# Hybrid attention trunk on one core: turned probabilities in two buffers with writes of their own, and DRAM reads emitted later

## The chip, the core and the metric

The kernel runs on one core of a Trainium2 chip. The metric is device time in microseconds for one execution of the whole program. Engines are named as the profile names them: PE (TensorE matmuls) and PEld (its weight loads), DVE (VectorE), ACT (ScalarE), POOL (GpSimd), SP (SyncE, which here issues nearly every DMA).

## What is computed

Two layers, each with a pooling mixer and a latent-attention mixer in parallel, over 512 tokens plus 16 meta tokens (T = 528), width 1024, 8 heads. Cut to what matters:

```python
for l in range(DEPTH):                      # DEPTH = 2
    h = rmsnorm(h_res, norm_gain[l])
    u_pool, z_pool, c_q, c_kv, k_rope, z_mla, g_pool, g_mla = split(h @ w_in[l])
    y_pool = (pool_mix(u_pool) * silu(z_pool)) @ pool_w_up[l]
    o_mla  = mla(c_q, c_kv, k_rope, ...)    # q, k normed and rotated; per head and block of
                                            # 128 queries: p = softmax(q k^T), causal; o = p v
    y_mla  = (o_mla * silu(z_mla)) @ mla_w_up[l]
    h_res += (sigmoid(g_pool) * y_pool + sigmoid(g_mla) * y_mla) @ w_out[l]
```

## The kernel before

**The matmul stream.** Every dense product is a `Gemm` in one list (`plan`), and `stream()` walks it: chunks of up to 512 weight columns, each loaded by `wload` (DMA `raw<-win` and the like on SP, line 133; high part `whi` on ACT, line 197; low part `wlo` on DVE, line 198) and multiplied by `mm3` in three passes (lines 202, 203, 204: high x high, high x low, low x high) to keep float32 accuracy. `raw`, `whi` and `wlo` have three buffers each. In layer 0 a chunk is 24 matmuls of 264 columns, in layer 1 it is 12 of 512.

**Attention woven into it.** `go()` runs the eight heads of a layer; between their pieces `gap()` lets the stream advance by some 2.6 us of planned matmul time (`FILL`), so that PE has dense work while DVE, ACT and the DMAs prepare a head. `after(ns, fn)` runs `fn` once the stream's own clock has advanced by `ns`. `behind(a, b)` makes instruction `a` wait for `b`; with `newest[0]` that is the last matmul emitted. Each engine runs its instructions in a fixed order. That order is not the program's: the framework's planner takes, per engine, what is ready in its own timing model, and among several the one that the program emitted first. At run time an engine, SP too, waits at the head of its queue.

**One head**, `head()`, blocks i = 0 to 3 of 128 queries, block i with 16 + 128(i+1) keys:

- First half: `scores` for block 1 (272 columns) and the first `SPL` = 240 columns of block 3 into one PSUM bank `sa`; block 2 (400 columns) into `sb`. `top` (DVE, line 824) scales, masks and takes the row maximum; `expo` (ACT, line 831) exponentiates into SBUF (`pa`, `cq`). A gap; then `turn` (DVE, line 837) transposes blocks 1 and 2 in 32x32 squares into `attD`; `pv` (lines 950, 953) multiplies an earlier head's probabilities with V; a gap.
- Second half: the other 288 columns of block 3, and block 0 (144 columns, in `passes`, line 872) into a bank `sc`; `top`, `expo` and `turn` for both. Then on SP: the row sums' reciprocals to DRAM (`rdr`, line 894), the four writes `pdr<-attD` (line 899), the read `attE<-pdr` that completes the turn (line 901), the broadcast read `cq<-rdr` (line 902). An odd head also writes and reads the meta tokens' probabilities (`mdr<-cq`, line 916; three `racc<-mdr`, line 918) and POOL multiplies the gates by the reciprocals (line 906).

`attD` has one buffer of 10 x 128 columns, `attE` has two. `parts(h)` (lines 928, 929) splits `attE` into high and low for `pv`; it comes four gaps after head h, with head h+1 in between. `prep` (lines 791 to 801) makes the next head's query and key tiles, largely by small SBUF-to-SBUF DMAs on SP.

PSUM has three banks with tag `S` (`sa`, `sb`, `sc` of a head in turn) and four with tag `mm`. `WARM` = 8 matmuls on ones (line 155) precede the first real matmul. `halves()` lends buffers, among them `attD` and `attE`, as scratch for squares before attention starts.

Of the kernel before, what the change touches and what calls it, by code (L numbers as in the profile page):

```python
# [9 lines left out]
F32 = mybir.dt.float32  # L10
F32R = mybir.dt.float32r
# [7 lines left out]
P = 128  # L19
DEPTH = 2  # L20
D = 1024
SEQ = 512
NM = 16
T = SEQ + NM
HALF = T // 2
# [28 lines left out]
RESERVE = ("gm3", "gm3")  # L54
LAG = 2000.0
TAIL = (9000.0, 9000.0)
SPL = 240
RET = 12500.0
WARM = 8
NB = 10  # L60


def block(i, j):
    return 2 * i + j if j < 2 else 1 if i == 2 else 6 + j
# [14 lines left out]
def trunk(ctx, tc, xT, xrow, mrow, pos, win, wkr, wqb, wkb, wvb, wgr, wpu, wmu, wout, gains, const, yT):  # L79
    nc = tc.nc  # L80
    pe, act, dve, gp, sp = nc.tensor, nc.scalar, nc.vector, nc.gpsimd, nc.sync
# [11 lines left out]
    def nm(s):  # L93
        uid[0] += 1
        return f"{s}_{uid[0]}"

    def slot(tag, dt=F32, bufs=1, w=W):
        return sl.tile([P, w], dt, tag=tag, name=nm(tag), bufs=bufs)
# [1 line left out]
    def tmp(w=W):  # L100
        return tp.tile([P, w], F32, tag="tmp", name=nm("tmp"), bufs=3)

    def att(tag):
        return sl.tile([P, NB * P], F32 if tag == "D" else F32R, tag=f"att{tag}", name=nm(f"att{tag}"), bufs=1 if tag == "D" else 2)

    def wide():
        return tp.tile([P, NB * P], F32R, tag="th", name=nm("th"), bufs=2)

    def halves():
        for k in range(4, 8):  # L110
            for a, b in FULL:
                yield xb[:, k, a:b]
        for tag in "DE":
            t = att(tag)
            for a in range(4):
                yield t[:, HALF * a:HALF * a + HALF].bitcast(F32)

    def mmt():
# [2 lines left out]
    def sct():  # L121
        return pp.tile([P, 512], F32, tag="S", name=nm("S"), bufs=3)
# [84 lines left out]
    newest = [None]  # L207
# [60 lines left out]
    def after(ns, fn):  # L268
        pend.append((clk[0] + ns, fn))
        pend.sort(key=lambda e: e[0])  # L270
# [32 lines left out]
    def behind(ins, other):  # L303
        tc.add_manual_dep(ins.ins, other.ins.name,
                          mybir.DependencyInfo(mybir.DependencyClass.Sync, mybir.DependencyReason.DATA))
# [35 lines left out]
    class Layer:  # L341
# [463 lines left out]
        def head(self, h, kq, prev):  # L805
            kh, kl, qh, ql = kq
            odd = h % 2
            nqs = self.nqs
            pa, pb, pc = slot("pa", w=416), slot("cq8"), slot("cq10")
            bia = sm.tile([P, 5], F32, tag="bia", name=nm("bia"), bufs=2)  # L810
            rs = sm.tile([P, 5], F32, tag="rs", name=nm("rs"), bufs=2)
            if odd == 0:
                self.pm = sm.tile([P, 4, 32], F32, tag="pm", name=nm("pm"), bufs=2)
                self.rb = slot("cq11")
            pm, rb = self.pm, self.rb
            blocks = att("D")
            grid = blocks.rearrange("p (b s r) -> p b s r", b=4, s=NB)

            def scores(i, out, a, b):
                q0 = NM + P * i  # L820
                return mm3(out, qh[:, q0:q0 + P], ql[:, q0:q0 + P], kh[:, a:b], kl[:, a:b], True, True)

            def top(i, c, sv, mask):
                return dve.tensor_tensor_reduce(out=sv, in0=sv, in1=mask, scale=nqs[:, i, h:h + 1], scalar=3e38,  # L824
                                                op0=ALU.add, op1=ALU.min, accum_out=bia[:, c:c + 1])

            def causal(n):
                return maskw[:, 512 - n:]

            def expo(i, c, sv, pv):  # L830
                act.activation(pv, sv, AF.Exp, scale=-1.0, bias=bia[:, i:i + 1], accum_out=rs[:, c:c + 1])  # L831

            def turn(i):
                gp.tensor_copy(pm[:, i, 16 * odd:16 * odd + 16], pt[i][:, 0:NM])  # L834
                for j, n in ((0, i + 1),) if i in (0, 1, 3) else ((0, 2), (2, 1)):
                    k = block(i, j)
                    ins = dve.transpose(grid[:, :, k:k + n, :].rearrange("p b s r -> p s b r"), pt[i][:, NM + P * j:NM + P * (j + n)])  # L837
                    if i in (1, 2):
                        behind(ins, newest[0])

            pt = [pa[:, 0:144], pa[:, 144:416], pb[:, 0:400], pc[:, 0:T]]
            sa = sct()
            s1, s3 = sa[:, 0:272], sa[:, 272:272 + SPL]
            scores(1, s1, 0, 272)
            scores(3, s3, 0, SPL)
            top(1, 1, s1, causal(272))
            top(3, 4, s3, maskw[:, 0:SPL])
            sb = sct()
            s2 = sb[:, 0:400]
            scores(2, s2, 0, 400)  # L850
            top(2, 2, s2, causal(400))
            expo(1, 1, s1, pt[1])
            expo(2, 2, s2, pt[2])
            if h == 1:
                self.spread_rope(1)
            if odd == 0 and h + 2 < H:
                self.spread_k(h // 2 + 1)
            self.gap()
            turn(1)
            turn(2)  # L860
            self.pv(prev)
            if h == 2:
                self.rope_keys(1)
            if odd and h + 1 < H:
                behind(self.keys(h // 2 + 1), newest[0])
            self.gap()
            sc = sct()
            s0, s4 = sc[:, 0:144], sc[:, 144:144 + T - SPL]
            scores(3, s4, SPL, T)

            def passes(out, q0, n):
                return [lambda k=k, q=q, x=x: pe.matmul(out, q[:, q0], x[:, 0:n], start=k == 0, stop=k == 2)
                        for k, (q, x) in enumerate(((qh, kh), (qh, kl), (ql, kh)))]

            todo = passes(s0, slice(NM, NM + P), 144)
            if not self.last:
                sm_ = sc[0:NM, 432:432 + NM]
                todo += passes(sm_, slice(0, NM), NM)
            for fn in todo:
                fn()  # L880
            if not self.last:
                dve.tensor_add(self.smeta[:, h, :], sm_, cst[0:NM, C_MM:C_MM + NM])
            top(3, 3, s4, causal(T - SPL))
            top(0, 0, s0, causal(144))
            dve.tensor_tensor(out=bia[:, 3:4], in0=bia[:, 3:4], in1=bia[:, 4:5], op=ALU.min)
            expo(3, 4, s3, pt[3][:, 0:SPL])
            expo(3, 3, s4, pt[3][:, SPL:T])
            expo(0, 0, s0, pt[0])
            turn(3)
            turn(0)  # L890
            dve.tensor_add(rs[:, 3:4], rs[:, 3:4], rs[:, 4:5])
            dve.reciprocal(rs[:, 0:4], rs[:, 0:4])
            row = rdr[self.l][h]
            sp.dma_start(row.rearrange("a (p i) -> p (a i)", i=4), rs[:, 0:4])
            got = att("E")
            n = NB * 32
            via = pdr[h % 2]
            for a in range(4):
                sp.dma_start(via[:, n * a:n * a + n].rearrange("(b k) x -> k b x", k=32),
                             blocks[32 * a:32 * a + 32, :].rearrange("p (b x) -> p b x", x=n))  # L900
            sp.dma_start(got.bitcast(F32), via)
            sp.dma_start(rb[64 * odd:64 * odd + 64, 0:512], row.partition_broadcast(64))
            if odd == 1:
                self.meta_turn(pm)
                z = self.zms[h // 2][:, NM:T].rearrange("p (i q) -> p i q", i=4)
                gp.tensor_mul(z, z, rb[:, 0:512].rearrange("p (q i) -> p i q", i=4))  # L906
            return h, got

        def meta_turn(self, pm):
            t = slot("cq9", F32R)  # L910
            f, hi, lo = t[:, 0:P], t[:, P:2 * P], t[:, 2 * P:3 * P]
            dve.transpose(f.bitcast(F32), pm.rearrange("p i r -> p (i r)"))
            split(hi, lo, f.bitcast(F32), 0, P)
            self.mt = slot("racc", F32R)
            via = mdr[0]
            sp.dma_start(via, t[:, P:3 * P].bitcast(F32))
            for g, c in ((0, 0), (32, 1), (64, 0)):
                sp.dma_start(self.mt[g:g + 32, 0:512].bitcast(F32).rearrange("p (a x) -> p a x", a=4),
                             via[:, P * c:P * c + P].rearrange("(a r) x -> r a x", a=4))

        def parts(self, prev):
            if prev is None:
                return None
            h, got = prev
            hi, f = wide(), got.bitcast(F32)
            for a in (0, NB * 64):
                b = a + NB * 64
                behind(act.activation(hi[:, a:b], f[:, a:b], AF.Copy), newest[0])  # L928
                dve.tensor_sub(got[:, a:b], f[:, a:b], hi[:, a:b].bitcast(F32))  # L929
            return h, hi, got  # L930
# [333 lines left out]
```

## Time and profile before

| | |
|---|---|
| median of 3 runs | 771.3 us (768.76 to 771.66) |
| the profiled execution's own time | 770.3 us |
| its span, first to last instruction | 768.5 us |
| DVE, ACT, POOL busy | 537.7, 393.3, 141.1 us |
| DMA | 113.03 MB, 48% of 16 engines' time |
| attention of layer 0, of layer 1 | from about 177 to 316 us, from about 564 to 695 us |

Times are microseconds from the span's start unless marked ns. Line numbers (L199) are lines of the kernel before. In a timeline row stand start, duration, engine and line, operation, output<-inputs, tile shape and count; in brackets the engine's idle time just before and what ended it. `SPq` marks an instruction of SP's queue, and its duration is the time that issuing took, not the transfer. In a row of the waits stand total, number and longest. A matmul's duration in a row includes the pipeline's depth: the distance from one start to the next is what it costs.

### The profile page before, as it was taken

How to read it: one execution, taken by the hardware profiler on the slowest of the kernel's cores; microseconds unless marked ns; L12 is line 12 of the kernel's file. 1: busy time of each engine (PE TensorE's matmuls, PEld its weight loads, DVE VectorE, ACT ScalarE, POOL GpSimd, SP SyncE). 2: the span in 40 equal slices, each digit the busy share in tenths (PEclk: the TensorE clock that was granted, in tenths of full speed). 3: DMA queues.
4: the chain of work that ended last, by engine and by line, in shares of the span. 5: the costliest groups of instructions: out<-in, count | busy, mean ns of one | idle time of the engine just before them, and what ended most of it. 6: DMA issues, size and time to landing. Idle time of an engine off the chain costs nothing.

```text
span 768.5 us, 14306 instructions
## 1 busy us (share of the span) xinstructions
PE 757.2 (99%) x5028; PEld 689.0 (90%) x5028; DVE 537.7 (70%) x1211; ACT 393.3 (51%) x864; POOL 141.1 (18%) x187
## 2 busy tenths in 40 slices
PE   9999999999999899999999999999999999999998
PEld 9999999999989899999997898887788788788887
DVE  4588787358889887684366477774578799776832
ACT  5755655545556555543255445455445556554320
POOL 2026404000101010052130264030001110112400
PEclk9999999999999999999999999999999999999999
DMA  7532323336765667425542323234457677673363
GB/s 261 181 109 84 100 80 104 118 124 165 200 201 164 179 201 204 141 83 147 177 143 93 114 83 100 80 89 132 127 158 197 197 207 206 187 214 105 121 196 108
DMA packets 77204, 113.03 MB, mean 147 GB/s; under 512 B 15382, under 2 KB 36246, under 8 KB 77132
## 3 DMA queue, kind: packets, MB, share of 16 engines
q1 hardware_dynamic: 76988, 111.86, 48.4%
q8 instruction: 39, 0.64, 0.3%
q14 instruction: 33, 0.27, 0.1%
q10 hardware_dynamic: 144, 0.26, 0.1%
HBM read 89.76 MB, written 15.86 MB: 137 GB/s over the span
## 4 chain that ended last, share of the span: by engine, by line
PE 85%; DVE 6%; DMA 5%; SPq 1%; issue 1%; ACT 1%; DVEq 0%; ACTq 0%
PE mm L202 26%; PE mm L204 25%; PE mm L203 25%; DMA raw<-win 2%; PE S L202 2%; PE S L204 2%; PE S L203 2%; DVE wlo L198 1%; DVE S L824 1%; DMA kh<-kh 1%; DMA pdr<-attD 1%; PE S L528 1%; PE o L950 1%; PE o L953 1%; DMA mdr<-cq 1%
## 5 line engine op out<-in xcount | busy, mean ns | idle before, releaser
L202 PE MATMUL mm<-hh,whi 128*128 128x264 f32 (+2 forms) x1072 | 338.9, 318 | 5.9 <-ACT whi L197 4.0
L204 PE MATMUL mm<-hh,wlo 128*128 128x264 f32 (+2 forms) x1072 | 338.4, 318 | 0.2 <-DVE wlo L198 0.2
L203 PE MATMUL mm<-hl,whi 128*128 128x264 f32 (+2 forms) x1072 | 337.9, 316 | 0.0
L198 DVE TENSOR_TENSOR wlo<-raw,whi 128x512 fp32r<-128x512 f32 (+2 forms) x242 | 172.5, 715 | 108.5 <-ACT whi L197 103.3
L197 ACT ACTIVATE whi<-raw 128x512 fp32r<-128x512 f32 (+2 forms) x242 | 144.4, 600 | 181.2 <-PE mm L203 126.8
L202 PEld LDWEIGHTS mm<-hh,whi 128*128 128x128 f32 x1072 | 202.7, 189 | 20.2 <-ACT whi L197 4.9
L203 PEld LDWEIGHTS mm<-hl,whi 128*128 128x128 f32 x1072 | 202.8, 189 | 12.4
L204 PEld LDWEIGHTS mm<-hh,wlo 128*128 128x128 f32 x1072 | 202.2, 189 | 12.7 <-DVE wlo L198 0.6
L834 POOL COPY pm<-cq 128x16 f32<-128x16 f32 x32 | 13.3, 416 | 216.5 <-ACT cq L831 216.5
L824 DVE CUSTOM_DVE_ANT_0 S<-S,maskw,nqs 128x240 f32<-128x240 f32 (+4 forms) x80 | 38.3, 499 | 2.3 <-PE S L204 1.7
L642 POOL TENSOR_TENSOR racc<-racc,tmp 128x264 f32<-128x264 f32 (+1 forms) x15 | 14.3, 957 | 134.8 <-ACT tmp L641 134.8
L1025 POOL TENSOR_TENSOR tmp<-tmp,xb 128x264 f32<-128x264 f32 (+1 forms) x24 | 27.1, 1142 | 55.2 <-DVE tmp L1023 53.3
L831 ACT ACTIVATE cq<-S,bia 128x400 f32<-128x400 f32 (+2 forms) x48 | 24.4, 512 | 25.0 <-DVE bia L824 11.9
L202 PE MATMUL mm<-cq,whi 128*128 128x264 f32 (+1 forms) x108 | 34.8, 322 | 0.0
L203 PE MATMUL mm<-th,whi 128*128 128x264 f32 (+1 forms) x108 | 34.7, 321 | 0.0
L202 PE MATMUL mm<-u,whi 128*128 128x264 f32 (+1 forms) x108 | 34.6, 321 | 0.0
L204 PE MATMUL mm<-cq,wlo 128*128 128x264 f32 (+1 forms) x108 | 34.6, 322 | 0.0
L203 PE MATMUL mm<-cq,whi 128*128 128x264 f32 (+1 forms) x108 | 34.6, 321 | 0.0
L204 PE MATMUL mm<-u,wlo 128*128 128x264 f32 (+1 forms) x108 | 34.5, 319 | 0.0
L837 DVE STREAM_TRANSPOSE attD<-cq 128x256 f32<-128x256 f32 (+2 forms) x48 | 21.3, 467 | 12.7 <-DMA pdr<-attD 7.2
L906 POOL TENSOR_TENSOR u<-u,cq 128x512 f32<-128x512 f32 x8 | 12.4, 1552 | 76.4 <-DMA cq<-rdr 26.9
L929 DVE TENSOR_TENSOR attE<-attE,th 128x640 fp32r<-128x640 f32 x32 | 25.1, 809 | 0.5 <-ACT th L928 0.5
(297 smaller groups left out, 1304.7 us busy)
## 6 DMA issues: line engine op xcount, KB each, us to landing
raw<-win SPq DMA_DIRECT2D x143, 256.0 KB, 3.3
pdr<-attD SPq DMA_DIRECT2D x64, 160.0 KB, 3.1
attE<-pdr SPq DMA_DIRECT2D x16, 640.0 KB, 4.9
raw<-wout SPq DMA_DIRECT2D x32, 256.0 KB, 2.9
raw<-wpu SPq DMA_DIRECT2D x16, 256.0 KB, 2.7
raw<-wmu SPq DMA_DIRECT2D x16, 256.0 KB, 2.5
raw<-wqb SPq DMA_DIRECT2D x12, 256.0 KB, 2.6
xb<-xT SPq DMA_DIRECT2D x8, 264.0 KB, 5.6
```

The source lines that it names most:

```text
L197: act.activation(hi[:, :n], raw[:, :n], AF.Copy)
L198: dve.tensor_sub(lo[:, :n], raw[:, :n], hi[:, :n].bitcast(F32))
L202: first = pe.matmul(out, wh, xh, start=start, stop=False)
L203: pe.matmul(out, wh, xl, start=False, stop=False)
L204: newest[0] = pe.matmul(out, wl, xh, start=False, stop=stop)
L642: self.acc_last = gp.tensor_add(self.acc[:, a:b], self.acc[:, a:b], t[:, :b - a])
L824: return dve.tensor_tensor_reduce(out=sv, in0=sv, in1=mask, scale=nqs[:, i, h:h + 1], scalar=3e38, op0=ALU.add, op1=ALU.min, accum_out=bia ...
L831: act.activation(pv, sv, AF.Exp, scale=-1.0, bias=bia[:, i:i + 1], accum_out=rs[:, c:c + 1])
L834: gp.tensor_copy(pm[:, i, 16 * odd:16 * odd + 16], pt[i][:, 0:NM])
L837: ins = dve.transpose(grid[:, :, k:k + n, :].rearrange("p b s r -> p s b r"), pt[i][:, NM + P * j:NM + P * (j + n)])
L929: dve.tensor_sub(got[:, a:b], f[:, a:b], hi[:, a:b].bitcast(F32))
L1025: gp.tensor_add(t[:, :b - a], t[:, :b - a], self.am[m][:, a:b])
```

## The change

- `attD` is split: `attC` (6 x 128 columns: blocks 0, 1, 2) and `attD` (4 x 128: block 3), one buffer each. Each is written to DRAM by four DMAs of its own (`away(0)`, `away(1)`), so eight writes per head for the same bytes. `away(0)` stands in the first half, behind `turn(1)`, `turn(2)` and `turn(0)`.
- Block 0 is scored in the first half: its three matmuls go into bank `sa`, beside blocks 1 and 3, after the `top` of both in program order. `SPL` falls from 240 to 96, so block 3 is cut into 96 and 432 columns.
- The reads back (`attE<-pdr`, `cq<-rdr`, then POOL's multiplication) are emitted by `after(BACK)`, 5200 ns of stream time later, each behind the newest matmul. An odd head's meta write is emitted 2600 ns later and its three reads 7800 ns later.
- `WARM` is 9. `halves()` lends other buffers, `attE` twice.

```diff
-SPL = 240
+SPL = 96
+BACK = 5200.0
-WARM = 8
+WARM = 9
...
-        for tag in "DE":
-            t = att(tag)
-            for a in range(4):
+        for tag, n in (("C", 6), ("D", 4), ("E", NB), ("E", NB)):
+            t = att(tag, n)
+            for a in range(n * P // HALF):
...
-                self.rb = slot("cq11")
-            pm, rb = self.pm, self.rb
-            blocks = att("D")
-            grid = blocks.rearrange("p (b s r) -> p b s r", b=4, s=NB)
+            pm = self.pm
+            blocks, grid = [], []
+            for tag, n in (("C", 6), ("D", 4)):
+                blocks.append(att(tag, n))
+                grid.append(blocks[-1].rearrange("p (b s r) -> p b s r", b=4, s=n))
+            n, via = NB * 32, pdr[h % 2]
+
+            def away(i):
+                x0, x1 = ((0, 192), (192, n))[i]
+                for a in range(4):
+                    sp.dma_start(via[:, n * a + x0:n * a + x1].rearrange("(b k) x -> k b x", k=32),
+                                 blocks[i][32 * a:32 * a + 32, :].rearrange("p (b x) -> p b x", b=4))
...
-                    if i in (1, 2):
+                    if i != 3:
                         behind(ins, newest[0])
...
-            s1, s3 = sa[:, 0:272], sa[:, 272:272 + SPL]
+            s1, s3, s0 = sa[:, 0:272], sa[:, 272:272 + SPL], sa[:, 368:512]
             scores(1, s1, 0, 272)
             scores(3, s3, 0, SPL)
             top(1, 1, s1, causal(272))
             top(3, 4, s3, maskw[:, 0:SPL])
+            for fn in passes(s0, slice(NM, NM + P), 144):
+                fn()
             sb = sct()
             s2 = sb[:, 0:400]
             scores(2, s2, 0, 400)
             top(2, 2, s2, causal(400))
+            top(0, 0, s0, causal(144))
             expo(1, 1, s1, pt[1])
             expo(2, 2, s2, pt[2])
+            expo(0, 0, s0, pt[0])
...
             turn(1)
             turn(2)
+            turn(0)
+            away(0)
             self.pv(prev)
...
-            s0, s4 = sc[:, 0:144], sc[:, 144:144 + T - SPL]
+            s4 = sc[:, 0:T - SPL]
             scores(3, s4, SPL, T)
...
-            expo(0, 0, s0, pt[0])
             turn(3)
-            turn(0)
...
+            got = []
+            away(1)
             sp.dma_start(row.rearrange("a (p i) -> p (a i)", i=4), rs[:, 0:4])
-            got = att("E")
-            n = NB * 32
-            via = pdr[h % 2]
-            for a in range(4):
-                sp.dma_start(via[:, n * a:n * a + n].rearrange("(b k) x -> k b x", k=32),
-                             blocks[32 * a:32 * a + 32, :].rearrange("p (b x) -> p b x", x=n))
-            sp.dma_start(got.bitcast(F32), via)
-            sp.dma_start(rb[64 * odd:64 * odd + 64, 0:512], row.partition_broadcast(64))
             if odd == 1:
                 self.meta_turn(pm)
-                z = self.zms[h // 2][:, NM:T].rearrange("p (i q) -> p i q", i=4)
-                gp.tensor_mul(z, z, rb[:, 0:512].rearrange("p (q i) -> p i q", i=4))
+
+            def back():
+                got.append(att("E"))
+                behind(sp.dma_start(got[0].bitcast(F32), via), newest[0])
+                if odd == 0:
+                    self.rb = slot("cq11")
+                rb = self.rb
+                behind(sp.dma_start(rb[64 * odd:64 * odd + 64, 0:512], row.partition_broadcast(64)), newest[0])
+                if odd == 1:
+                    z = self.zms[h // 2][:, NM:T].rearrange("p (i q) -> p i q", i=4)
+                    gp.tensor_mul(z, z, rb[:, 0:512].rearrange("p (q i) -> p i q", i=4))
+
+            after(BACK, back)
             return h, got
...
-            self.mt = slot("racc", F32R)
             via = mdr[0]
-            sp.dma_start(via, t[:, P:3 * P].bitcast(F32))
-            for g, c in ((0, 0), (32, 1), (64, 0)):
-                sp.dma_start(self.mt[g:g + 32, 0:512].bitcast(F32).rearrange("p (a x) -> p a x", a=4),
-                             via[:, P * c:P * c + P].rearrange("(a r) x -> r a x", a=4))
+
+            def back():
+                self.mt = slot("racc", F32R)
+                for g, c in ((0, 0), (32, 1), (64, 0)):
+                    ins = sp.dma_start(self.mt[g:g + 32, 0:512].bitcast(F32).rearrange("p (a x) -> p a x", a=4),
+                                       via[:, P * c:P * c + P].rearrange("(a r) x -> r a x", a=4))
+                    behind(ins, newest[0])
+
+            after(BACK / 2, lambda: behind(sp.dma_start(via, t[:, P:3 * P].bitcast(F32)), newest[0]))
+            after(1.5 * BACK, back)
```

More of the change, by code (lines that the diff above doesn't have):

```diff
@@ L101, in tmp, with att @@
         return tp.tile([P, w], F32, tag="tmp", name=nm("tmp"), bufs=3)
-    def att(tag):
-        return sl.tile([P, NB * P], F32 if tag == "D" else F32R, tag=f"att{tag}", name=nm(f"att{tag}"), bufs=1 if tag == "D" else 2)
+    def att(tag, n=NB):
+        return sl.tile([P, n * P], F32 if tag != "E" else F32R, tag=f"att{tag}", name=nm(f"att{tag}"), bufs=1 if tag != "E" else 2)
     def wide():
@@ L835, in turn @@
                 for j, n in ((0, i + 1),) if i in (0, 1, 3) else ((0, 2), (2, 1)):
-                    k = block(i, j)
-                    ins = dve.transpose(grid[:, :, k:k + n, :].rearrange("p b s r -> p s b r"), pt[i][:, NM + P * j:NM + P * (j + n)])
-                    if i in (1, 2):
+                    g, k = grid[i // 3], block(i, j) - 6 * (i // 3)
+                    ins = dve.transpose(g[:, :, k:k + n, :].rearrange("p b s r -> p s b r"), pt[i][:, NM + P * j:NM + P * (j + n)])
+                    if i != 3:
                         behind(ins, newest[0])
@@ L847, in head, with passes @@
             top(3, 4, s3, maskw[:, 0:SPL])
+            def passes(out, q0, n):
+                return [lambda k=k, q=q, x=x: pe.matmul(out, q[:, q0], x[:, 0:n], start=k == 0, stop=k == 2)
+                        for k, (q, x) in enumerate(((qh, kh), (qh, kl), (ql, kh)))]
+            for fn in passes(s0, slice(NM, NM + P), 144):
+                fn()
             sb = sct()
@@ L867, in head @@
             sc = sct()
-            s0, s4 = sc[:, 0:144], sc[:, 144:144 + T - SPL]
+            s4 = sc[:, 0:T - SPL]
             scores(3, s4, SPL, T)
[L871 to L875, printed above, removed]
             if not self.last:
                 sm_ = sc[0:NM, 432:432 + NM]
[L878 to L881, printed above, removed]
+                for fn in passes(sm_, slice(0, NM), NM):
+                    fn()
                 dve.tensor_add(self.smeta[:, h, :], sm_, cst[0:NM, C_MM:C_MM + NM])
             top(3, 3, s4, causal(T - SPL))
-            top(0, 0, s0, causal(144))
             dve.tensor_tensor(out=bia[:, 3:4], in0=bia[:, 3:4], in1=bia[:, 4:5], op=ALU.min)
@@ L924, in parts @@
             h, got = prev
+            got = got[0]
             hi, f = wide(), got.bitcast(F32)
```

## The prediction

> **What bounds the kernel now.** I begin with busy time by engine and the list of what PE waited for.
>
> ```profile
> PE 757.2 (99%) x5028; PEld 689.0 (90%) x5028; DVE 537.7 (70%) x1211; ACT 393.3 (51%) x864; POOL 141.1 (18%) x187
> ```
> ```profile
> PE mm L202 <- ACT whi L197: 4.0, 3, 1.9
> PE mm L202 <- DVE tmp L655: 1.8, 1, 1.8
> ```
>
> PE is the bound: nothing off PE can save more than PE's holes. The second view has almost all of them: three waits for a weight's high part, 4.0 us in all, the longest 1.9 and the others about 1.0 each, and one of 1.8 us for an eviction. All four lie in attention. Next, the stretches around the two longest, with PE's granted clock as the column after the engines:
>
> ```profile
> 257.00:270.00 13.00, 10.95 (x75) 10.44 (x74) 11.76 (x30) 7.78 (x19) 0.39 (x2) 0.87 0.58 168
> 594.00:608.00 14.00, 12.11 (x50) 9.93 (x50) 9.98 (x25) 5.99 (x14) 3.22 (x5) 0.88 0.71 203
> ```
> ```profile
> 601.10:604.40 3.30, 3.30 (x11) 2.84 (x10) 3.30 (x11) 3.22 (x10) 0.99 (x2) 0.50 0.27 81
> ```
>
> After each of the two the clock falls: the means 0.87 over 13 us and 0.88 over 14 us are 1.7 us lost each, and the third row shows it at 0.50, PE busy throughout. So the four holes cost 4.0 + 1.8 + 2 x 1.7 = 9.2 us. *A rule beside it:* the Trainium skill, "TensorE: Matmul & The Clock Gate", section "Why this matters for your kernels", warns only of idle gaps over about 3 us. By it these holes would cost 5.8 us and the sum below would end 3.4 us higher; the 0.50 after holes of 1.8 and 1.9 us says otherwise, and I go by the row.
>
> Why are they there? SP's queue before the longest (PE stops at about 598.5):
>
> ```profile
> 583.66 0.34 SPq L133 DMA_DIRECT2D raw<-win  x1
> ```
> ```profile
> 588.61 2.01 SPq L899 DMA_DIRECT2D pdr<-attD  x4
> ```
> ```profile
> 593.18 0.34 SPq L901 DMA_DIRECT2D attE<-pdr  x1
> 593.57 0.52 SPq L801 DMA_DIRECT2D qhl<-q  x1
> 594.20 1.50 SPq L918 DMA_DIRECT2D racc<-mdr  x3
> 595.74 0.51 SPq L801 DMA_DIRECT2D qhl<-q  x1
> 596.30 1.83 SPq L133 DMA_DIRECT2D raw<-win  x3
> ```
> ```profile
> 599.89 0.63 ACT L197 ACTIVATE whi<-raw 128x512 fp32r<-128x512 f32 x1 [6.60 <-DMA raw<-win]
> ```
>
> For 12.6 us no weight is loaded, then three in a row: their buffers had been free. SP was busy issuing an odd head's burst (writes, reads back, the meta exchange, the next head's queries) and standing at its head. ACT sits 6.60 us without weights, and PE runs dry. The stall for an eviction comes the other way, over DVE:
>
> ```profile
> SPq L902 <- DMA rdr<-rs: 17.3, 10, 2.8
> SPq L918 <- DMA mdr<-cq: 17.1, 6, 3.6
> ```
> ```profile
> SPq L901 <- DMA pdr<-attD: 9.2, 12, 1.3
> ```
> ```profile
> DVE attD L837 <- DMA pdr<-attD: 9.8, 5, 3.0
> ```
> ```profile
> 257.49 0.64 DVE L837 STREAM_TRANSPOSE attD<-cq 128x256 f32<-128x256 f32 x2 [2.56 <-PE S L872]
> ```
>
> SP stands 17.3 + 17.1 + 9.2 = 43.6 us before reads whose writes have not landed. DVE stands 9.8 us because the one `attD` is still being written out; just before the 1.8 us hole it stood 2.56 us at the same instruction.
>
> **The change part by part.**
>
> *The two buffers.* Blocks 0 to 2 are written out in the first half, so the next head's first `turn` finds `attC` long free, and block 3's buffer has half a head to drain. The 12.4 us of DVE's waiting go; the hole behind them (1.8, and 1.7 of clock) goes with it. Next late there would be `wlo`, which has DVE's freed time. DVE, ACT and POOL get the same number of instructions over the same columns; block 0's `top`, `expo` and `turn` only swap halves with 144 columns of block 3.
>
> *The later reads.* 16 `attE`, 16 `cq` and 24 `racc` reads and 8 meta writes are emitted after the weight loads of two gaps, so the planner prefers those loads. I count the three weight holes as gone: 4.0 + 1.7 us. The new waits on PE stand in SP's queue before these reads; behind them wait weight loads and `prep`'s copies. Each names a matmul that was newest at emission, two gaps after the head, which is about where the next head's first scores stand. In the rows above and below these run at 588.5 and the read is issued at 593.18: its writes land later than that matmul ends. I take nothing for the new waits; above, they keep SP standing as today, and one hole of 1.0 us stays in each layer, 2 us.
>
> *Four more writes per head.*
>
> ```profile
> pdr<-attD SPq DMA_DIRECT2D x64, 160.0 KB, 3.1
> attE<-pdr SPq DMA_DIRECT2D x16, 640.0 KB, 4.9
> ```
>
> The bytes stay, in pieces of 96 and 64 KB, and only the reads wait for their landing, 3.1 us today. From the row at 588.61, 0.50 us of SP each: 64 x 0.50 = 32 us over both layers, against 43.6 us of standing that the later reads can save. Half of them go out in the first half, away from the burst. Nothing on PE, as long as no load is pushed out by over its lead; if that cover goes, a weight hole returns (1.0 us, or 1.9 with 1.7 of clock).
>
> *Matmuls.* Start to start, in layer 1:
>
> ```profile
> 588.46 0.27 PE L204 MATMUL S<-kh,qhl 96*128 96x240 f32 x1
> 588.57 0.35 PE L202 MATMUL S<-kh,qhl 96*128 96x400 f32 x1
> 588.75 0.34 PE L203 MATMUL S<-kl,qhl 96*128 96x400 f32 x1
> ```
> ```profile
> 593.14 0.39 PE L204 MATMUL mm<-hh,wlo 128*128 128x512 f32 x1
> 593.37 0.30 PE L202 MATMUL S<-kh,qhl 96*128 96x288 f32 x1
> 593.50 0.30 PE L203 MATMUL S<-kl,qhl 96*128 96x288 f32 x1
> ...
> 593.77 0.23 PE L872 MATMUL S<-kh,qhl 96*128 96x144 f32 x1
> 593.84 0.28 PE L872 MATMUL S<-kl,qhl 96*128 96x144 f32 x1
> 593.95 0.27 PE L872 MATMUL S<-kh,qhl 96*128 96x144 f32 x1
> 594.06 0.44 PE L202 MATMUL mm<-hh,whi 128*128 128x512 f32 x1
> ```
>
> 240 columns cost 0.11 us, 288 0.13, 400 0.18, 512 0.23; 144 cost 0.07 once and then 0.11, no less than 240, so narrow passes are bounded by something other than columns. 432 lies between 400 and 512: 0.197. The 96 has no row: below, 0.045 by columns (0.05 per 112 from 400 to 512); above, 0.11 as a follow-on 144. Per head, three passes each: 240 + 288 + 144 took 0.33 + 0.39 + 0.29 = 1.01 us; 96 + 144 + 432 take 0.33 + 0.29 + 0.59 = 1.21 at the upper end and 1.02 at the lower. Times 16: +0.2 to +3.2 us. The 144 is the nearest row, so I take +2.8.
>
> *The ninth warm-up matmul.*
>
> ```profile
> 1.05 3.78 PE L155 MATMUL wps<-ones 128*128 128x128 f32 x16 [1.05 <-DVE na L754]
> 5.18 0.99 PE L202 MATMUL S<-hh,th 128*128 128x264 f32 x2 [0.35 <-ACT hh L364]
> ```
>
> Eight take 3.4 us up to their successor, 0.43 each; a ninth fills the 0.35 us hole and runs over by 0.1. Bounds: +0.43 if nothing hides it; -1.7, one half-clock stretch as above, if an unbroken start brought the full clock one stretch earlier. I take +0.1.
>
> *Sum.* -9.2 + 2.8 + 0.1 = -6.3. Every engine's order is planned anew, and I leave one hole of about 0.8 us in: -5.5. The profiled execution took 770.3 us (span 768.5), 1.0 below the median of 771.3; from the median, **765.8 us**.
>
> **The rivals.**
>
> *PE waits for DVE at block 0 (slower).* Block 0's matmuls now write the bank in which `top` of blocks 1 and 3 works, and come after both. Does the program order work on one bank whose columns differ? Yes:
>
> ```profile
> 624.84 0.51 DVE L824 CUSTOM_DVE_ANT_0 S<-S,maskw,nqs 128x272 f32<-128x272 f32 x1
> ...
> 627.77 0.46 DVE L824 CUSTOM_DVE_ANT_0 S<-S,maskw,nqs 128x240 f32<-128x240 f32 x1
> ```
> ```profile
> 628.39 0.49 ACT L831 ACTIVATE pa<-S,bia 128x272 f32<-128x272 f32 x1 [1.66 <-DVE bia L824]
> ```
>
> Block 1's `expo` reads columns finished at 625.4 and still sits 1.66 us until block 3's `top`, in the same bank, is done. The Trainium skill ("PSUM — Partial Sum Buffer", section "PSUM bank collisions raise a hardware error") asks just that: guard by bank, not by address. So PE, in fixed order with the whole stream behind those three matmuls, will wait for DVE once per head where the planner has placed them too early. For: in these rows the second `top` ends 2.9 us behind the first, whose columns were scored together; such lags are long and uneven. Against: PE depends on DVE for every `wlo` and many evictions, and the list of its waits has one DVE entry of weight, 1.8 us, so the planner's places mostly hold. It decides from 0.35 us a head, which eats the gain; at 0.9 us a head, 14.4 us: **780 us**.
>
> *The reads come too late for `parts` (slower).*
>
> ```profile
> 670.29 0.34 SPq L901 DMA_DIRECT2D attE<-pdr  x1
> ```
> ```profile
> 675.54 1.37 ACT L928 ACTIVATE th<-attE 128x640 fp32r<-128x640 f32 x2
> ```
>
> That read, 4.9 us in the median, had 5.25 us. If a read falls 2 to 3 us further back, ACT stands with `whi` queued behind it; at 0.7 us of it per head on PE, 11 us: **777 us**. Against: today's reads wait for writes, not for their place.
>
> *The change doesn't do what it says.* As shown, the due point is past before the writes land, so the reads may keep their place in the burst, while 32 us of writes are added. Then only DVE's hole goes: -3.5 + 2.8 + 0.1, **770.7 us**.
>
> **How the numbers follow.** Forecast 0.50 (759 to 768: all holes gone and 96 columns at the lower end, up to one long hole left); no later reads 0.25 (768 to 774); PE waiting for DVE 0.15 and late reads 0.10 (774 to 783). A measurement of this kernel tells about 0.5% from no change, so faster is below 767.4 and slower above 775.2. Faster: 0.48 of the forecast and 0.04 of the third, 0.52; slower: 0.20 of the two slower ones and 0.03 of the third, 0.23; same: 0.25. Range for 8 in 10: 758, with the clock bound of the warm-up in it, to 779.
>
> **What would show it.** Right: no clock of 0.50 in attention, PE's waits for `whi` and `tmp` under 2 us in all, DVE's wait at L837 for `pdr` gone, loads of `raw` between the writes and the read of one head, SP's waits before the reads well under 43.6 us. The matmul term: the start-to-start distance of the 96. Wrong: PE's waits name `top` before the 144 columns, or ACT waits for `attE`, or SP shows over 10 us without a `raw` load again.

## The result and the profile after

The changed kernel takes 774.94 us in the median (772.98 to 778.06), the kernel before 770.36 us beside it: a ratio of **1.0069, 95% interval 1.0052 to 1.0085**, slower by 4.0 to 6.5 us. 765.8 us was forecast. The profiled executions took 770.3 us before and 778.06 us after, at the upper end of its runs, so the traces differ by more (7.8 us) than the medians do (4.6).

Busy time by engine, on the page of after:

```profile
PE 760.3 (98%) x5030; PEld 686.9 (88%) x5030; DVE 538.3 (69%) x1211; ACT 394.4 (51%) x864; POOL 142.9 (18%) x187
```

PE's idle time is span less busy: 768.5 - 757.2 = 11.3 us before, 776.3 (the span of after) - 760.3 = 16.0 after. So of the 7.8 us, 3.1 are more busy time and 4.7 more idle time. Where they lie shows when both traces are read at the same matmul of the stream. When attention of layer 0 begins, the changed kernel is 2.2 us ahead (its clock rose earlier at the start of that execution, see the last section); when that attention has ended it is 1.0 ahead, at the end of layer 1's 7.8 behind. So 8.8 of the 10.0 us that attention loses are lost in layer 1, where PE's idle time grew from 3.1 to 7.2 us.

What PE waited for (total, times, longest). In rows of the changed kernel and of the experiments, line numbers are lines of that version: L203 is here what L202 was before.

```profile
PE mm L203 <- ACT whi L198: 4.4, 5, 2.0
PE S L203 <- DMA kh<-cq: 3.4, 3, 1.7
PE S L203 <- issue: 1.6, 1, 1.6
...
PE o L973 <- DVE attE L949: 1.0, 1, 1.0
PE S L205 <- DMA qhl<-q: 0.6, 1, 0.6
```

The eviction's 1.8 us is gone, the weight holes are not (4.0 before, 4.4 now), and a kind of wait that hardly stood in the list of before (0.6 us) is new: scores wait for `prep`'s key and query copies, DMAs in SP's queue. (`issue` means that the profile shows nothing that PE waited for in those 1.6 us.) So SP comes next. Its timeline around the longest `whi` hole, in layer 0, and PE's row behind it:

```profile
254.86 1.05 SPq L134 DMA_DIRECT2D raw<-win  x2
256.01 0.50 SPq L798 DMA_DIRECT2D kl<-kl  x1
256.56 3.09 SPq L825 DMA_DIRECT2D pdr<-attC  x4
...
260.86 0.55 SPq L800 DMA_DIRECT2D kh<-cq  x1
...
264.88 3.23 SPq L825 DMA_DIRECT2D pdr<-attD  x4
...
269.46 0.32 SPq L911 DMA_DIRECT2D attE<-pdr  x1
...
274.25 1.62 SPq L134 DMA_DIRECT2D raw<-win  x3
```
```profile
263.94 0.54 PE L203 MATMUL S<-kh,qhl 96*128 96x272 f32 x2 [1.69 <-DMA kh<-cq]
```
```profile
278.11 0.39 PE L203 MATMUL mm<-hh,whi 128*128 128x264 f32 x1 [2.03 <-ACT whi L198]
```

No weight is loaded from the second of the pair at 254.86 until 274.25, 18.8 us from issue to issue. The key copy of 260.86, for which PE waits until 263.94, stands behind the four writes of `attC` (3.09 us of issuing); four of `attD` follow (3.23 us), and the next loads come so late that PE stops for 2.03 us at 278.11. The same stretch of the kernel before:

```profile
251.15 0.57 SPq L133 DMA_DIRECT2D raw<-win  x1
251.83 0.39 SPq L899 DMA_DIRECT2D pdr<-attD  x1
...
252.75 1.58 SPq L899 DMA_DIRECT2D pdr<-attD  x3
...
257.12 0.54 SPq L133 DMA_DIRECT2D raw<-win  x1
257.83 0.34 SPq L901 DMA_DIRECT2D attE<-pdr  x1
258.23 3.28 SPq L133 DMA_DIRECT2D raw<-win  x2
```

There loads stand on both sides of the writes. In 6 of layer 1's 8 heads the writes of after do not even stand in two places. One head on four engines (PE, ACT, DVE, SP):

```profile
571.43 0.29 PE L203 MATMUL S<-kh,qhl 128*128 128x272 f32 x1
...
578.24 0.35 PE L203 MATMUL S<-kh,qhl 128*128 128x432 f32 x1
...
578.82 0.23 PE L859 MATMUL S<-kh,qhl 128*128 128x144 f32 x1
```
```profile
581.09 0.47 ACT L840 ACTIVATE pa<-S,bia 128x272 f32<-128x272 f32 x1
```
```profile
582.38 0.62 DVE L846 STREAM_TRANSPOSE attC<-pa 128x256 f32<-128x256 f32 x2
583.12 0.67 DVE L846 STREAM_TRANSPOSE attD<-cq 128x512 f32<-128x512 f32 x1
```
```profile
588.56 2.00 SPq L825 DMA_DIRECT2D pdr<-attC  x4
590.66 1.86 SPq L825 DMA_DIRECT2D pdr<-attD  x4
```

Block 0's 144 columns were to be scored in the first half. They run at 578.82, behind block 3's 432, in the second; so they do in 9 of the 16 heads. Block 1's `expo` shares a bank with them and waits: 9.7 us behind its scores here, 11.3 in the median against 6.7 before. Both buffers are filled at the same moment, and all eight writes leave in a row. Between the loads at 583.56 and 599.49 lie 15.9 us, at this place 12.6 before. The writes are not the whole of it: in between SP also stands, ahead of a key copy, for 3.7 us (2.7 before):

```profile
SPq L800 <- DMA kh<-kh: 3.7, 1, 3.7
```

The clock (the column after the engines) at the two places shown of before, then of the half-speed stretch in the second, and behind the 2.03 us hole:

```profile
257.00:270.00 13.00, 11.31 (x89) 10.89 (x88) 11.80 (x31) 7.17 (x18) 0.39 (x2) 1.00 0.56 162
594.00:608.00 14.00, 11.75 (x50) 9.61 (x49) 9.62 (x27) 7.85 (x20) 2.36 (x5) 0.88 0.82 226
602.10:605.50 3.40, 3.40 (x11) 3.02 (x11) 2.56 (x8) 3.23 (x10) 0.64 (x3) 0.50 0.78 245
```
```profile
278.20:281.60 3.40, 3.31 (x25) 3.10 (x26) 3.03 (x9) 3.40 (x12) 0.71 (x3) 1.00 0.44 137
```

### The profile page after: what moved, and what is told of

It reads as the page before. It is cut to its first block, busy times and chain, and to the rows that moved or that the text cites. A ratio compares the mean times of both kernels' runs of the same rounds, so it can differ in the third digit from the quotient of the medians.

```text
span 776.3 us, 14420 instructions
## 1 busy us (share of the span) xinstructions
PE 760.3 (98%) x5030; PEld 686.9 (88%) x5030; DVE 538.3 (69%) x1211; ACT 394.4 (51%) x864; POOL 142.9 (18%) x187
## 4 chain that ended last, share of the span: by engine, by line
PE 84%; DMA 8%; DVE 3%; SPq 2%; ACT 1%; issue 1%; POOL 0%; DVEq 0%; ACTq 0%
PE mm L205 25%; PE mm L203 25%; PE mm L204 25%; DMA raw<-win 4%; PE S L203 2%; PE S L204 2%; PE S L205 2%; DMA kh<-cq 1%; DMA kh<-kh 1%; PE o L973 1%; PE o L970 1%; DMA attE<-pdr 1%; DVE wlo L199 1%; PE S L529 1%; ACT whi L198 1%
## 5 line engine op out<-in xcount | busy, mean ns | idle before, releaser
L203 PE MATMUL mm<-hh,whi 128*128 128x264 f32 (+2 forms) x1072 | 337.9, 317 | 4.4 <-ACT whi L198 4.4
L199 DVE TENSOR_TENSOR wlo<-raw,whi 128x512 fp32r<-128x512 f32 (+2 forms) x242 | 174.8, 726 | 118.7 <-ACT whi L198 113.6
L203 PEld LDWEIGHTS mm<-hh,whi 128*128 128x128 f32 x1072 | 201.7, 189 | 19.1 <-ACT whi L198 6.2
L204 PEld LDWEIGHTS mm<-hl,whi 128*128 128x128 f32 x1072 | 201.9, 188 | 12.6
L833 DVE CUSTOM_DVE_ANT_0 S<-S,maskw,nqs 128x144 f32<-128x144 f32 (+4 forms) x80 | 38.2, 497 | 3.8 <-PE S L859 1.8
L203 PE MATMUL mm<-cq,whi 128*128 128x264 f32 (+1 forms) x108 | 34.8, 322 | 0.0
L203 PE MATMUL mm<-u,whi 128*128 128x264 f32 (+1 forms) x108 | 34.6, 320 | 0.0
L948 ACT ACTIVATE th<-attE 128x640 fp32r<-128x640 f32 x32 | 21.9, 730 | 12.3 <-DMA attE<-pdr 8.0
```

Source lines behind the costliest of these rows:

```text
L199: dve.tensor_sub(lo[:, :n], raw[:, :n], hi[:, :n].bitcast(F32))
L203: first = pe.matmul(out, wh, xh, start=start, stop=False)
L204: pe.matmul(out, wh, xl, start=False, stop=False)
```

## The experiments

Ratios are to the kernel before, measured beside each version on the same chip. In the expectations, "burst theory", later "SP theory", is that SP's long run of issues at a head's end costs the time; its rivals are the narrower matmuls, the later reads, the order of work in one bank, and chance in the planner's new order. "Without a load" means from one weight load's issue to the next within attention, its first 20 us or so aside, where every version has a long one.

**Undoing one part of the changed kernel.** First the place of block 0's matmuls in program order, ahead of the two `top`s that work in their bank:

```diff
             scores(3, s3, 0, SPL)
+            for fn in passes(s0, slice(NM, NM + P), 144):
+                fn()
             top(1, 1, s1, causal(272))
             top(3, 4, s3, maskw[:, 0:SPL])
-            for fn in passes(s0, slice(NM, NM + P), 144):
-                fn()
```

> The changed kernel with block 0's three matmuls emitted ahead of the two tops that work in the same bank, so that PE need not come back to that bank after DVE. Burst theory (block 0 sits in a bank with blocks 1 and 3, the planner places its matmuls late, the first half's writes slide to the second half's, and SP issues eight writes in a row while key copies and weight loads wait): the four first-half writes come some microseconds ahead of the others again, the PE waits for key copies go, ratio to before about 1.000 (0.996 to 1.003). Matmul rival (narrower passes, 2.2 us of PE time, plus chance): stays near 1.006. Late-reads rival (reads emitted 5.2 us later starve the parts step): stays near 1.006.

Measured: 777.12 us, 1.0018 (0.9989 to 1.0048). Block 0 is late in one head, and block 1's `expo` lags 7.0 us:

```profile
573.16 0.21 PE L203 MATMUL S<-kh,qhl 96*128 96x96 f32 x1
...
573.43 0.30 PE L855 MATMUL S<-kh,qhl 96*128 96x144 f32 x1
```
```profile
576.86 0.49 ACT L840 ACTIVATE pa<-S,bia 128x272 f32<-128x272 f32 x1 [0.45 <-DVE bia L833]
```

The 144 columns stand right behind the 96, and some 0.5% comes back. Next, in the changed kernel, all reads and the meta exchange are emitted at once again (`back()` in place of `after(BACK, back)`, without `behind`):

> The changed kernel with every read back and the meta exchange emitted at once, as before the change. Late-reads rival: the gain comes back, ratio to before about 1.001, ACT's waits for attE (8.0 us in the changed kernel) gone. Burst theory: the burst of eight writes plus reads is as long or longer, ratio 1.006 to 1.012. Matmul rival: about 1.006.

Measured: 785.32 us, 1.0137 (1.0092 to 1.0181), PE waiting 7.0 us for `whi`. So the later reads are not what the change costs; here it is dearer without them.

**One part alone in the kernel before.** The later reads; the scoring (`SPL` = 96, block 0 in bank `sa`, one `attD`, four writes); the two buffers with eight writes at the head's end:

> The kernel before with only the later emission of the reads and of the meta exchange; one attD, four writes, block 0 in the second half. Late-reads rival: most of the loss is here, ratio 1.004 to 1.007. Burst theory: no loss, 0.995 to 1.001, since weight loads go ahead of the reads. Matmul rival: 1.000.

> The kernel before with only the scoring moved: block 0 in the first half beside blocks 1 and 3, SPL 96, one attD, four writes, reads at once. Matmul rival: 2.2 us of PE, ratio 1.003, and most of the loss if the rest of it is chance. Burst theory: 2.2 us plus a little, 1.002 to 1.005: without the four extra writes the late first half costs less than in the changed kernel. Late-reads rival: 1.000 to 1.003.

> The kernel before with the two buffers and eight writes alone; block 0 in the second half, so all eight writes stand at the head's end, reads at once. SP theory: 32 us more of issuing in the burst, ratio 1.003 to 1.010, with waits for whi and key copies. If only the bank order matters: 0.996 to 1.001, as DVE no longer waits for attD.

Measured: 775.09 us, 1.0001 (0.9974 to 1.0029); 787.0 us, 1.0162 (1.0119 to 1.0205); 789.25 us, 1.0175 (1.014 to 1.0211). Scoring and eight writes each cost more alone than the whole change, and more than either had been expected to. A part of it is the clock: in the profiled execution with the eight writes it was granted at 0.50 for 34.1 us of attention in all, in that with the scoring for 13.7, in the kernel before for 6.8. The scoring with `a_bank`'s order on top of it:

> As d_score_only (scoring moved alone, ratio 1.016 there), with block 0's three matmuls emitted ahead of the two tops of their bank. Burst theory in its new form (the bank order is what makes the moved scoring dear: exp of block 1 lags its scores by 11 us instead of 7): the ratio falls to 1.002 to 1.007, the lag to about 7 us. Matmul rival (narrow passes plus chance): stays at 1.010 or above.

Measured: 784.0 us, 1.0101 (1.0055 to 1.0147), with block 1's lag down from 11.4 to 7.3 us. The bank's order is a part of the scoring's cost, 0.6% (the two intervals overlap), and not the whole.

**Are the writes' issues the cost?** `attC`'s four writes go to POOL's queue, without and with the order of `a_bank`:

```diff
-                    sp.dma_start(via[:, n * a + x0:n * a + x1]
+                    (sp if i else gp).dma_start(via[:, n * a + x0:n * a + x1]
```

> The changed kernel with the four writes of attC issued from POOL's queue instead of SP's, so SP issues 64 DMAs less; the scoring order is the changed kernel's. SP theory (what costs is the length of SP's burst): ratio to before 0.998 to 1.003, PE's waits for key copies and whi fall by half. Bank-order-only theory (the late first half itself starves PE): stays at 1.005 to 1.009.

> a_bank (block 0's matmuls ahead of the tops, 1.002) with the four writes of attC issued from POOL: SP issues five per head, as in the kernel before. SP theory: 0.990 to 0.998, as m_bank_two. If POOL's queue is a poor place for them (its copies of the meta columns stand behind, as i_pool's 1.012 suggests): 1.002 to 1.010.

Measured: 784.04 us, 1.0117 (1.0081 to 1.0152), and 775.37 us, 0.9993 (0.9969 to 1.0017). Fewer issues on SP alone bring nothing; SP theory missed in the first and fell just short in the second. Then the DRAM buffer is laid out anew, so that a half's write is one DMA from all 128 partitions and the read is four pieces:

```diff
-                for a in range(4):
-                    sp.dma_start(via[:, n * a + x0:n * a + x1].rearrange("(b k) x -> k b x", k=32),
-                                 blocks[i][32 * a:32 * a + 32, :].rearrange("p (b x) -> p b x", b=4))
+                sp.dma_start(via.rearrange("(b p) x -> p b x", b=4)[:, :, x0:x1],
+                             blocks[i].rearrange("p (b x) -> p b x", b=4))
```

with `a_bank`'s order, in the changed kernel, in the kernel before (one write, four reads), and in that with the later reads:

> a_bank (the changed kernel, block 0's matmuls ahead of the tops; 1.002) with the DRAM buffer laid out so that each half's write is one DMA and the read is four: six issues per head on SP instead of nine. SP theory: 0.993 to 0.999, better than both kernels. If SP's issues are not what costs: 1.000 to 1.004, as a_bank.

> The changed kernel, bank order untouched, with the DRAM buffer laid out so that each half's write is one DMA and the read four: six issues per head on SP instead of nine. SP theory (the number of issues in the burst at a head's end): 0.996 to 1.002. Bank-order theory (late first half is what costs, whatever SP issues): 1.005 to 1.010. If both are needed: about 1.003.

> The kernel before with the same DRAM layout: one write and four reads, five issues as before. A control: SP theory says 0.997 to 1.003, since the number of issues stands. If the layout itself is the gain of m_bank_two (0.990), for instance because the turned blocks land sooner, 0.988 to 0.995.

> c_reads_only (the kernel before with only the later reads, 1.000) with that layout: one write, four reads, later. Without the moved scoring it saves its 2.3 us of narrow passes. If layout and later reads are what helps in m_bank_two: 0.985 to 0.992. If the two buffers are needed: 0.996 to 1.002.

Measured: 768.6 us, 0.9903 (0.9866 to 0.9941); 772.95 us, 0.9976 (0.9952 to 1.0); 769.92 us, 0.9908 (0.9874 to 0.9943); 765.9 us, **0.985 (0.9813 to 0.9887)**. Four pairs, each 0.9 to 1.5% faster than its partner without the layout (1.0018, 1.0069, 1, 1.0001). PE's waits for `whi` are 0.0, 1.9, 0.4 and 0.0 us in the four, against 0.2, 4.4, 4.0 and 8.0 in the partners. The mere number of issues isn't what the layout saves: the third issues five DMAs per head for this exchange, as the kernel before does, and SP theory had put it at 0.997 to 1.003. The last is the fastest version and beats both kernels. SP in it, at the place that the prediction showed of before:

```profile
583.48 0.53 SPq L898 DMA_DIRECT2D pdr<-attD  x1
...
587.00 0.58 SPq L134 DMA_DIRECT2D raw<-win  x1
...
588.20 1.84 SPq L905 DMA_DIRECT2D attE<-pdr  x4
...
590.61 1.06 SPq L134 DMA_DIRECT2D raw<-win  x2
```

One write of 0.53 us, and loads between it and its read. Is it the single write or the reads in pieces? The same layout, but the write again in four DMAs (each one group of 128 columns from all partitions):

> The kernel before with the regrouped DRAM buffer, but the write stays four DMAs (now one per group of 128 columns, each from all 128 partitions) and the read is four: eight issues of SP where the version with one write had five. If the gain of 0.9% came from the reads in four pieces with loads between them, or from writes that touch all 128 partitions, it stays here (0.989 to 0.994). If it came from the write being one issue, so that the last byte leaves 1.5 us earlier, this one is at 0.998 to 1.006, SP standing less but issuing 2 us more per head.

Measured: 775.61 us, 1.0038 (1.0016 to 1.006), 1.3% above the version with one write, which is more than any edit that does nothing moved the time (next paragraph). The reads in pieces bring nothing; the single write does.

**What does any new order bring?** Every edit makes the planner order all engines anew. Two versions of the kernel before that do the same work (one with a ninth warm-up matmul), the changed kernel with its warm-up undone, and both kernels at a second `FILL`:

> The kernel before with FILL at 2600 and 2510 in place of 2620 and 2530: the same work, and the stream's chunks stand at slightly other places between the pieces of attention, so every engine gets a new order. If the differences of the parts (-0.9 to +1.75%) are what any new order brings by chance, this one lies as far out: below 0.99 or above 1.01. If they come from the mechanisms named, this one lies between 0.995 and 1.005, with waits for whi on PE of 2 to 7 us.

> The kernel before with a ninth warm-up matmul alone. By the prediction's term +0.1 us, at most +0.43 (1.0000 to 1.0006); -1.7 us (0.998) if it brought the full clock a stretch earlier. If a new order alone moves the time, it lies outside 0.995 to 1.005.

> The changed kernel with eight warm-up matmuls as before the change. If the ninth is worth nothing, the changed kernel's 1.007 stays (1.004 to 1.010). If the 0.7% is the chance of one order, it lies anywhere from 0.995 to 1.02.

> The kernel before with FILL at 2640 and 2550: the other direction from the version with 2600 and 2510, which took 1.0075. If the FILL of before stands in a narrow optimum, this one is at 1.003 to 1.010 too; if a new order moves the time to either side by chance, it may lie below 1 (0.993 to 1.01).

> The changed kernel with FILL at 2640 and 2550. If the change has a cost of its own, this one stands 0.5 to 1% above the kernel before with the same FILL; if its 0.7% is what any new order brings, the two stand anywhere to each other, within 1% either way.

Measured: 778.44 us, 1.0075 (1.0044 to 1.0106) for `FILL` 20 ns lower; 772.65 us, 0.9982 (0.9957 to 1.0007) for `WARM` = 9; 778.86 us, 1.008 (1.0048 to 1.0112) for the changed kernel with `WARM` = 8; at `FILL` 20 ns higher 770.96 us, 0.9998 (0.9975 to 1.0022) for the kernel before and 775.64 us, 1.0059 (1.0035 to 1.0083) for the changed one. The first is the most sobering: 20 ns of `FILL`, which nothing asks for, cost as much as the whole change, PE's waits for `whi` rising from 4.0 to 8.3 us:

```profile
PE mm L202 <- ACT whi L197: 8.3, 4, 2.6
```

So one difference of 0.7% proves no mechanism. What holds is what repeats: the changed kernel stands at 1.006 to 1.008 in three orders, the kernel before at 0.998 to 1.0075 in four, with only one of the four as high; and the layout pays in each of four pairs.

**One view that divides the versions.** The number of stretches over 13.1 us without a load; the bound was chosen afterwards, between 13.0 in v_fill_up and 13.2 in d_score_only:

| stretches | versions and ratios |
|---|---|
| none | the kernel before 1, o_reads_one 0.985, m_bank_two 0.9903, n_before_one 0.9908, m_after_two 0.9976, g_warm 0.9982, k_bank_pool 0.9993, v_fill_up 0.9998, a_bank 1.0018 |
| 1 or 2 | c_reads_only 1.0001, s_four_writes 1.0038, u_fill 1.0075, j_score_first 1.0101, i_pool 1.0117 |
| 3 | w_after_fill 1.0059, **the changed kernel 1.0069**, t_warm8 1.008, d_score_only 1.0162 |
| 4 | b_reads_now 1.0137, e_two_bufs 1.0175 |

Of all versions with none, the slowest is at 1.0018; of those with any, all but one are at 1.0038 or more. With 14 us as the bound only s_four_writes changes sides; with 12.5, the kernel before, g_warm and v_fill_up do. Among the versions with such stretches their number doesn't order the ratios, and this is a correlation: no run lengthened a stretch and left all else alone. SP's issuing time in attention (177 to 312 us and 566 to 690 us) does not divide them so: it is 131.9 us in u_fill, 133.7 in d_score_only and 136.8 in the kernel before, but 141.4 in o_reads_one. An estimate of the limit: three buffers of `raw` and three of `whi` and `wlo` hold six chunks, each 12 x 0.23 = 2.8 us of PE in layer 1, 16.6 us together; the next load must land (3.3 us for `raw<-win`) and be converted (0.6 us, as `whi`) before they are used up, which leaves some 12.7 us, longer where attention's matmuls stand between. It is no sharp limit: the stretch of 12.6 us in the kernel before ends in its hole of 1.9 us.

## Why the prediction was wrong, point by point

**The step that failed** is the cost of the eight writes: "Half of them go out in the first half, away from the burst. Nothing on PE, as long as no load is pushed out by over its lead", and with it "I count the three weight holes as gone". Neither half came true. In 6 heads of layer 1 and 2 of layer 0 they go out in a row; in 3 of the other 8, as at 256 to 268, `prep`'s copies lie between them and no load. Each kind is seen to push a load out by over its lead (583 to 599 and 255 to 274), the case in which I had said that a hole returns. For the new waits behind SP's burst I took nothing; PE waited 4.0 us for key and query copies. Two buffers with eight writes alone cost 1.75%; the changed kernel with two writes in place of eight (and its read in four pieces) is at 0.9976. The forecast was -5.5 us, +4.6 came: matmuls as forecast, and nothing saved of the 9.2 us of holes, since waits for weights stayed and key and query copies joined them; in the traces PE's idle time grew by 4.7 us. That the eight writes alone make the 4.6 us isn't shown, since an edit that does nothing moved the time as far; that they did not spread and that the holes stayed is.

**The two buffers.** That DVE's 9.8 us for `pdr` would go, and PE's `tmp` hole with it, was right: of the ten versions with two buffers one has such a hole (0.9 us in k_bank_pool), of the ten with one buffer all but s_four_writes. But the 2.56 us that I added to make 12.4 are another wait: their row names a matmul of block 0's scores, not a write. "Blocks 0 to 2 are written out in the first half" was wrong, by the rival's own mechanism: work in one bank keeps its order. I looked for it in PE's waits for DVE's `top`, and the list has none of weight. The planner, which works with that order, places the matmuls late instead; the price appears as a late `expo` and a late write. a_bank gives back 0.5%, j_score_first 0.6%, m_bank_two against m_after_two 0.7%, k_bank_pool against i_pool 1.2%. The first three are no larger than what a new order brings by itself; all four go the same way.

**The later reads.** That they keep their place in the burst, the third rival, was right: issued 6.4 us behind block 3's `turn` in the median before, 5.4 after. Alone they are worth 0.0%. Late reads as a cost fall with b_reads_now, though in `parts` ACT and DVE do wait for them now, and PE once, for 1.0 us (`parts` stands five gaps behind its head, one more than said above):

```profile
L949 DVE TENSOR_TENSOR attE<-attE,th 128x640 fp32r<-128x640 f32 x32 | 26.6, 848 | 10.0 <-ACT th L948 10.0
...
L948 ACT ACTIVATE th<-attE 128x640 fp32r<-128x640 f32 x32 | 21.9, 730 | 12.3 <-DMA attE<-pdr 8.0
```

SP's standing before the reads fell from 43.6 us to 15.3, as I had said; that PE would have nothing of it I had not:

```profile
SPq L911 <- DMA pdr<-attD: 8.0, 14, 1.8
...
SPq L933 <- DMA mdr<-cq: 3.9, 4, 1.7
```

(3.4 us more stand at L915 for `rdr`.) An SP that stands holds up loads only if one is queued behind it and due; o_reads_one stands 27.1 us for `pdr` and is the fastest.

**The writes' own rows** were sized right, 2.00 us of SP for four:

```profile
attE<-pdr SPq DMA_DIRECT2D x16, 640.0 KB, 5.5
pdr<-attC SPq DMA_DIRECT2D x64, 96.0 KB, 2.7
pdr<-attD SPq DMA_DIRECT2D x64, 64.0 KB, 1.8
```

**Matmuls.** +2.8 us forecast. The narrow passes of all heads take 16.8 us start to start before and 19.3 after, +2.5:

```profile
589.43 0.21 PE L203 MATMUL S<-kh,qhl 96*128 96x96 f32 x1
589.48 0.27 PE L204 MATMUL S<-kl,qhl 96*128 96x96 f32 x1
589.59 0.28 PE L205 MATMUL S<-kh,qhl 96*128 96x96 f32 x1
589.70 0.41 PE L203 MATMUL S<-kh,qhl 96*128 96x400 f32 x1
```

The first 96 costs 0.05 us, the other two 0.11 each, as a 144 does.

**The clock.** I charged 1.7 us behind each long hole. It is no fixed price: behind the 2.03 us hole at 278 the rows above show 1.00, behind the two short holes that end at 600.77 and 601.90 they show 0.50 for 3.4 us. The Trainium skill ("TensorE: Matmul & The Clock Gate", section "Why this matters for your kernels") warns of idle gaps over about 3 us; the half-speed stretches here follow shorter ones, yet not each of them.

**The warm-up.** +0.1 forecast, with a bound of -1.7; both pairs (0.9982 for the kernel before, 1.0069 to 1.008 for the changed one) are within what a measurement here can tell.

**What stays open.** Why d_score_only keeps 1% that a_bank's order doesn't return (the narrow passes are 0.3% of it; its PE waits 9.8 us for `whi` and 6.8 for key copies, which says what, not why), and how a single write, with SP standing longer before its read than four did, gives the loads their places: the order that the planner makes of it was seen, its reason was not taken apart.

## What to carry to other kernels

Where one queue carries both the weights and a small exchange, count the longest stretch in which it issues no weight load and set it against what the buffers hold; the queue's busy time and its standing told less here. Splitting a transfer to start half of it early pays only if that half's last input is early as well; here a layout that makes four writes one was worth 0.9 to 1.5%, and the change's rescheduling nothing. And before a change of 0.7% is explained in a kernel whose order a planner makes, measure an edit that does nothing: here one of three moved the time as far.

## What was not expected of the hardware

Four writes of 160 KB, each from 32 partitions, held SP for 2.01 us and landed in 3.1 us each; one write of the same 640 KB from 128 partitions held it for 0.38 us in the median (0.53 in the row above) and landed in 4.7 to 4.9 us. One issue took 0.43 to 0.45 us in the median for 64, 96 and 160 KB, from 32 partitions or from 128, so over these sizes issuing is paid by the DMA and not by the byte. On POOL's queue an issue took 0.55 us.

The clock at the start isn't set by the number of warm-up matmuls alone. With eight of them the first 264-column matmuls of the changed kernel (t_warm8, the first rows) run 0.12 us apart, those of the kernel before (the second) 0.22, and it stays so until 10.6 us. That is why the changed kernel's trace is ahead at first; g_warm (nine) and v_fill_up (eight) also show 0.12 to 0.13 at this place, so it is not the ninth matmul that did it.

```profile
5.71 0.28 PE L204 MATMUL S<-hl,th 128*128 128x264 f32 x1
5.83 0.28 PE L205 MATMUL S<-hh,th 128*128 128x264 f32 x1
```
```profile
5.97 0.42 PE L203 MATMUL S<-hl,th 128*128 128x264 f32 x1
6.19 0.42 PE L204 MATMUL S<-hh,th 128*128 128x264 f32 x1
```
